# Value and forget-gate projections as one seven-product Strassen step, spatial mixing in plain fp32, and queries kept unnormalised, in a one-core decoder block

## The chip, the core and the metric

The kernel runs on one core of a Trainium2 chip. The metric is the device time of one execution in microseconds (us). Besides the timed runs there is one execution that was recorded by the hardware profiler; all rows of the profile and the trace come from that one. Its line numbers (L265) are those of the kernel before. Engines are named as in the profile: PE is TensorE (matmul), PEld its weight loads, DVE VectorE, ACT ScalarE, POOL GpSimd, SP the engine whose queue issues nearly all DMAs.

## The reference, cut to what matters

One decoder block, 1024 tokens by 1024 features, all float32:

```python
xn = rmsnorm(h, norm_mix_g)                 # 1024 tokens x 1024
proj = xn @ w_in                            # 1024 x 2568
q, k, v = proj[:, :512], proj[:, 512:1024], proj[:, 1024:1536]
log_f = log_sigmoid(proj[:, 2560:2568] + b_forget)     # 8 forget gates
att = forgetting_attention(q, k, v, log_f)  # softmax(q k^T / 8 + c_q - c_k, causal) v, 8 heads of 64
uv = gelu(proj[:, 1536:2560])               # u and gate, 512 columns each
sg = u * (w_spatial @ rmsnorm(gate) + b)    # per chunk of 128 tokens and group of 64 columns
h = h + concat(att, sg) @ w_out
h = h + conv_ffn(rmsnorm(h))                # up projection, causal convolution, silu gate, down
out = rmsnorm(h)
```

c is the running sum of log_f over the tokens. The change touches the projections of v and of the forget gates, the mixing `w_spatial @ ...`, and where q gets its per-token factor.

## The kernel before

**Products.** A float32 product is made of three fast matmuls (type fp32r): each operand is split into a high part (an ACT copy that rounds to fp32r) and a low part (a DVE subtraction, source minus high), and high x high, high x low and low x high are summed in PSUM. `tsplit` (L251) makes the two parts of a weight tile in a ring of six buffers (`ring`, L199: two tagged wy, four whl); `tmul` (L259) issues 4 x 3 matmuls for one of four 128-row blocks of the contraction, so that a product over 512 rows of contraction, for 512 tokens, is 48 matmuls. Their width is that of the weight tile: 512, 264 or 256 columns.

**Strassen steps.** With the two halves of the tokens and the two halves of the features, the input x is a 2 x 2 block matrix. The kernel keeps split blocks B11, B21 and B22 of it and the combinations T1 to T4, in the dictionary `XS`; tile tags H, V, x1, x2, t2, t3 hold them in turn. u and gate together (L284 to L419), queries and keys (`qk_step`, L594, four steps of 7 products of 12 matmuls 512 wide), the up projection and the down projection are each done with seven block products in place of eight.

**Values and forget gates before.** The 520 columns (512 values, 8 gates) are not done by a Strassen step, but as 8 products of 48 matmuls. Columns 0 to 255 of the values and the 8 gates (264 wide): `values_low` (L300) for the first half of the tokens, B11 and B21, interleaved block by block between the second and the third product of u and gate; `values_high` (L485) for the second half of the tokens, T3 and B22, behind u and gate; its weight sums are made on POOL (L487). Columns 256 to 511 (256 wide): T3, B11, B21, B22 (L810 to L850) behind the queries and keys, with weights `w0` split at L661 and the sums of L815 split at L845. `keep` (L304) copies the first results out of PSUM and writes them to DRAM (`vd`), `kept` (L696) loads them back; `evac_v` (L684) scales a result by the token's factor `rstd1` and splits it into the tile V (one ACT activation, one DVE operation for 256 columns of 128 tokens); all 16 are done ahead of the attention.

**Gate and mixing before.** `gate_part` and `gate_norm` (L465, L472) make the group norms of the gate and scale it, in the neighbourhood of `values_high`. `gate_gain` (L640) multiplies by the gain. `gate_split` (L667) splits the gate into high and low parts in four tiles of tag H; `spatial_weights` (L735) masks the mixing weights on POOL (L738) and splits them. `spatial` (L744) then issues for each of the 8 groups three fp32r matmuls 512 wide (L754 to L756), a DVE operation that adds the bias and multiplies with u (L759), and an ACT activation and a POOL product for the other half of the tokens. `turn_sg` (L775) transposes the result on PE (L780).

**Queries before.** In `emit` (L570) DVE multiplies queries and keys by the factor of the token (`rb`, a broadcast of rstd1 through DRAM, `rbd`, L403 to L405; queries also by -1/8), ACT makes the high part, DVE the low part, SP writes both to DRAM (`qd`, `kd`). `head_loads` (L823) brings them back per head. `logits_mm` (L914) makes the logits with a second matmul of 66 rows, of which rows 64 and 65 carry the running sums of the gates (`oned`, `ncd`); `logits_min` (L924) adds the causal mask and takes the row minimum in one DVE operation.

**What sets the order.** The framework orders each engine's instructions by a list schedule: by place in the program among those that it takes to be ready, and each queue then runs in that fixed order. `Line` (L30) overrides it: while `act.on` or `dve.on` is set, ACT or DVE runs its instructions in the order of the program, and `after` and `behind` put one instruction behind another without a wait between engines. Before the change this is on up to L402 and from L746 to L1060. `gates["keys"]` and `gates["queries"]` (L616, L633) are the last DVE operations on PSUM of the last query and key step; the splits of `w0` and `gate_gain` are put behind them. Buffers of one tag are reused in turn, and the DMA or instruction that writes a new tile waits for the last reader of the old one.

## Time and profile before

| | us |
|---|---|
| median of 3 runs (lowest, highest) | 1054.91 (1054.14, 1054.94) |
| profiled execution, its own time | 1053.8 |
| its span, first to last instruction | 1052.1 |
| PE busy | 1041.9 |
| DVE busy | 884.1 |
| ACT busy | 569.7 |
| POOL busy | 233.8 |
| u and gate, last two products (71.53 to 93.29) | 21.76 |
| `values_high` (93.29 to 104.92) | 11.63 |
| queries and keys (104.92 to 181.71) | 76.79 |
| columns 256 to 511 of the values (181.71 to 205.11) | 23.40 |
| mixing and first transposes (205.11 to 214.08) | 8.97 |

Times in the trace count from the start of the span. A row of the timeline gives start, duration, engine, line, operation, output and input tiles, and the number of instructions merged; the bracket at its end is the engine's idle time before it and what ended that. A row of the windows gives, for a stretch, its length, the busy time (and number of instructions) of each engine, the granted clock, the DMA share and GB/s. A row of the groups gives count, busy time and mean ns. A matmul's duration in a row is longer than its distance from the next one, because matmuls are pipelined; costs are therefore taken from the distance.

### The profile page before, as it was taken

Reading aid. Unit: us, or ns where it says so; the run is one execution under the profiler, and the core shown is the slowest. Engines: PE = TensorE matmul, PEld = TensorE weight load, DVE = VectorE, ACT = ScalarE, POOL = GpSimd, SP = SyncE. Lnnn points to the kernel's source line nnn. Section 1 sums busy time; section 2 is a strip of 40 time slices with the busy share of each in tenths; the row PEclk is TensorE's granted clock in tenths of the full one; section 3 lists DMA queues with packets and bytes.
Section 4 is the critical chain, followed back from the end, with each engine's and each line's share of the span. In section 5 each row is a group of like instructions: output and inputs, shape, how many; then the busy total and the mean of one; then the engine's idle time right before and its main releaser. Section 6 shows DMA issues by size and latency. Waiting matters only on the chain.

```text
span 1052.1 us, 14351 instructions
## 1 busy us (share of the span) xinstructions
PE 1041.9 (99%) x5037; PEld 873.8 (83%) x5037; DVE 884.1 (84%) x1293; ACT 569.7 (54%) x1008; POOL 233.8 (22%) x177
## 2 busy tenths in 40 slices
PE   9999999999999999999999999999999999999997
PEld 6989888988888888888888888888888888888886
DVE  6998797777787779998999989899897866997774
ACT  6777544456766746654344344444444554454654
POOL 0003231520421640253333423323331000000000
PEclk9999999999999999999999999999999999999999
DMA  9623456855755444222255332332322999333432
GB/s 332 214 8 134 139 154 172 230 145 181 191 159 163 152 163 157 80 90 90 80 180 170 120 113 78 131 120 69 131 82 80 316 329 303 103 100 100 144 119 98
DMA packets 67471, 155.77 MB, mean 148 GB/s; under 512 B 9060, under 2 KB 10036, under 8 KB 67400
## 3 DMA queue, kind: packets, MB, share of 16 engines
q1 hardware_dynamic: 66088, 154.82, 46.5%
q8 instruction: 39, 0.64, 0.3%
q14 instruction: 32, 0.26, 0.1%
q10 hardware_dynamic: 1312, 0.04, 0.1%
HBM read 111.96 MB, written 42.87 MB: 147 GB/s over the span
## 4 chain that ended last, share of the span: by engine, by line
PE 95%; DVE 2%; ACT 1%; issue 1%; DMA 0%; SPq 0%; ACTq 0%
PE k L1548 20%; PE qc L1288 11%; PE qa L1288 11%; PE qd L1288 11%; PE ps L265 6%; PE pb L265 5%; PE qb L1288 5%; PE pb L984 3%; PE pb L968 2%; PE qa L430 2%; PE qc L430 2%; PE qd L430 2%; PE pl L920 1%; PE pl L921 1%; PE pf L1008 1%; PE pf L1009 1%
## 5 line engine op out<-in xcount | busy, mean ns | idle before, releaser
L1548 PE MATMUL k<-whb,wha 128*128 128x512 f32 (+1 forms) x936 | 209.9, 386 | 0.0
L1548 PEld LDWEIGHTS k<-whb,wha 128*128 128x128 f32 x936 | 174.1, 188 | 35.8 <-DVE wha L161 0.2
L1288 PE MATMUL qc<-xT,whb 128*128 128x512 f32 x540 | 129.9, 389 | 0.2 <-ACT whb L155 0.2
L1288 PE MATMUL qa<-xB,wha 128*128 128x512 f32 x528 | 127.4, 390 | 0.0
L1288 PEld LDWEIGHTS qc<-xT,whb 128*128 128x128 f32 x540 | 101.3, 188 | 21.6 <-ACT whb L155 0.6
L1288 PEld LDWEIGHTS qa<-xB,wha 128*128 128x128 f32 x528 | 98.8, 188 | 20.8 <-DVE wha L161 0.4
L155 ACT CAST wha<-sg 128x512 fp32r<-128x512 f32 x77 | 47.7, 622 | 97.0 <-PE k L1548 86.5
L155 ACT CAST whb<-sg 128x512 fp32r<-128x512 f32 x82 | 50.6, 618 | 86.1 <-PE qc L1288 65.9
L161 DVE TENSOR_TENSOR wha<-sg,wha 128x512 fp32r<-128x512 f32 x77 | 52.7, 687 | 38.4 <-ACT wha L155 38.3
L1288 PE MATMUL qd<-xB,whb 128*128 128x512 f32 x264 | 63.7, 389 | 0.0
L1288 PE MATMUL qd<-xT,whb 128*128 128x512 f32 x264 | 63.7, 389 | 0.0
L969 ACT CAST pt<-pb 128x512 fp32r<-128x512 f32 x72 | 40.5, 585 | 41.5 <-PE pb L968 36.0
L1172 POOL TENSOR_TENSOR sg<-raw 128x512 f32<-128x512 f32 x20 | 30.8, 1539 | 139.9 <-DVE whb L161 79.9
L1288 PE MATMUL qb<-xT,whb 128*128 128x512 f32 x252 | 61.0, 389 | 0.0
L161 DVE TENSOR_TENSOR whb<-sg,whb 128x512 fp32r<-128x512 f32 x82 | 57.0, 697 | 4.4 <-ACT whb L155 4.3
L970 DVE TENSOR_TENSOR pt<-pb,pt 128x512 fp32r<-128x512 f32 x72 | 47.9, 688 | 15.1 <-ACT pt L969 15.0
L1288 PEld LDWEIGHTS qd<-xT,whb 128*128 128x128 f32 x264 | 49.5, 188 | 10.5 <-DVE u L1395 0.3
L1288 PEld LDWEIGHTS qd<-xB,whb 128*128 128x128 f32 x264 | 49.5, 188 | 10.3
L1288 PEld LDWEIGHTS qb<-xT,whb 128*128 128x128 f32 x252 | 47.2, 188 | 10.1 <-DVE whb L161 0.3
L984 PE MATMUL pb<-pt,V 128*128 128x512 f32 (+3 forms) x192 | 49.6, 362 | 0.4 <-DVE pt L970 0.3
L1175 POOL TENSOR_TENSOR sg<-sg,raw 128x512 f32<-128x512 f32 x20 | 33.3, 1665 | 63.4 <-DVE whb L161 63.4
L1173 POOL TENSOR_TENSOR sg<-sg,raw 128x512 f32<-128x512 f32 x20 | 35.1, 1757 | 47.2 <-issue 44.6
(417 smaller groups left out, 2267.0 us busy)
## 6 DMA issues: line engine op xcount, KB each, us to landing
raw<-wup SPq DMA_DIRECT2D x44, 512.0 KB
sg<-hx SPq DMA_DIRECT2D x77, 256.0 KB
hx<-hs SPq DMA_DIRECT2D x44, 256.0 KB
hx<-ca SPq DMA_DIRECT2D x35, 256.0 KB
xT<-wdn SPq DMA_DIRECT2D x28, 256.0 KB
x<-kd SPq DMA_DIRECT2D x24, 256.0 KB
A<-xtok SPq DMA_DIRECT2D x8, 512.0 KB
raw<-wqk SPq DMA_DIRECT2D x8, 512.0 KB
```

The costliest lines, as they stand in the source:

```text
L155: act.copy(h, src)
L161: return eng.tensor_tensor(out=l, in0=src, in1=f32(h), op=ALU.subtract)
L265: pe.matmul(banks[m], xs(n, xi, k)[:, ms], w[:, wi, :], start=(first and k == 0 and c == 0 and (own or m % 2 == 0)), stop=(k == 3 and c == ...
L430: pe.matmul(ps, w[:, wi, ks], xs(n, xi, k), start=(first and c == 0), stop=(c == 11), skip_group_check=True)
L969: casts.append(act.copy(pt[:, 0, :], ptr))
L970: los.append(dve.tensor_tensor(out=pt[:, 1, :], in0=ptr, in1=f32(pt[:, 0, :]), op=ALU.subtract))
L984: seq(pe.matmul(po[half][:, o:o + w], lhs, pt[:, s, c:c + w], start=(new and s == 0), stop=(s == 1 and (half, k) in ((1, 6), (0, 3))), ski ...
L1172: pool.tensor_tensor(out=s[0], in0=a21, in1=a22, op=ALU.add)
L1173: pool.tensor_tensor(out=s[1], in0=s[0], in1=a11, op=ALU.add)
L1175: pool.tensor_tensor(out=s[3], in0=s[1], in1=a12, op=ALU.add)
L1288: pe.matmul(ps, w[:, wi, ks], xb[:, xi, k, :], start=(first and n == 0), stop=(n == 11), skip_group_check=True)
L1548: pe.matmul((banks[bk + m] if ps is None else ps)[:, o], xh[:, xi, ms], wh[:, wi, o], start=((first and p_ == 0 or new) and n == 0), stop= ...
```

## The change: what it does

- **Values and forget gates become one Strassen step** of seven products. The two first, B11 and B21 (264 wide), stand where `values_low` stood, one after the other: the four blocks of B11, a copy of its result to DRAM (`vx[0]`), then the four of B21 into the same banks. Two, T3 and B22 (264 wide), stand where `values_high` stood; their weight sums are made by DVE (`vsum`) from tiles `va` and `v3rd` that hold both column halves of the weights (two loads of 128 x 1824 and one of 128 x 512 floats, in place of 1.1 MB), and their results go to DRAM (`vx[1]`, `vx[2]`). Three, T2, T4 and T1 (256 wide, `vmul`), stand behind queries and keys; their sums with the stored results (`xy`, `xl`, loaded back) give three blocks of values, two of which go through DRAM (`vu`).
- **Order.** DVE and ACT keep the program's order (`on`) also from L402 to the first query product; the gate norms, the splits and the subtractions are written out in one sequence there. The POOL sums for the first query weights are put behind the last low part of that sequence (`behind_`).
- **Mixing** takes the gate and the masked weights unsplit, as plain fp32: two matmuls 256 wide for each group in place of three fp32r ones 512 wide. `gate_split` and the split of the mixing weights go.
- **Queries** are no longer multiplied by the token's factor in `emit`; the factor (-rstd/8) is the scale of the DVE operation in `logits_min`, the mask changes sign, and the second logits matmul has 67 rows, with ncd rows prepared for both sides.
- **8 of the 16 `evac_v`** (heads 4 to 7) move into the attention, one in each of the steps 5 to 12.

```diff
-    values_low(0)
+    for k in range(2):
+        tmul(half(B), low_w(0, k), "B11", k, True)
     t2_of(0)
...
+    w12 = [low_w(1, k) for k in range(4)]
     for m in range(4):
         dve.tensor_tensor(out=ut[0][:, m, :], in0=S[m], in1=vgt[0][:, m, :], op=ALU.add)
-    values_low(3)
+    copies(B, vx[0])
+    for k in range(4):
+        tmul(half(B), w12[k], "B21", k, False)
...
-    act.on = dve.on = False
+    act.on = False
     rb = sb("t01", [P, 1024])
     act.dma_start(out=rbd.rearrange("a p -> p a"), in_=rstd1)
     sp.dma_start(out=rb, in_=rbd.rearrange("a b -> (a b)").unsqueeze(0).to_broadcast((P, 1024)))
+    act.on = True
+    gms = cst.tile([P, 64], F32, name="gms")
     XS["B22"] = xset(("t3", "t2"))
+    va = [sb("G", [P, 1824]) for _ in range(2)]
+    v3rd = sb("gg", [P, 512])
+    for i in range(2):
+        sp.dma_start(out=va[i], in_=wva[i])
+    sp.dma_start(out=v3rd, in_=wvk)
...
+    def vsum(i):
+        dve.tensor_tensor(out=own_[i][:, 0:3, 0:256], in0=oth[i], in1=own_[i][:, 0:3, 0:256], op=ALU.add)
+        dve.tensor_tensor(out=own_[i][:, 3, 0:256], in0=v3rd[:, 256 * i:256 * i + 256], in1=own_[i][:, 3, 0:256], op=ALU.add)
...
+    for k in range(4):
+        tmul(B, w4[k], "B22", k, False)
+    vsum(0)
+    sq = [square(1, 0), square(1, 2)]
+    w3 = [high(own_[0][:, k, :], 264) for k in range(2)]
+    reduce(sq[0], 1, 0)
     for m in range(4):
-        gelu(vgt[1][:, m, :], 4 + m)
         dve.tensor_tensor(out=vgt[0][:, m, :], in0=ut[1][:, m, :], in1=S[m], op=ALU.add)
         gelu(vgt[0][:, m, :], m)
+    for k in range(2):
+        low(w3[k], own_[0][:, k, :])
+    reduce(sq[1], 1, 2)
+    w3 += [high(own_[0][:, k, :], 264) for k in (2, 3)]
+    sq = [square(0, 0), square(0, 2)]
+    dve.tensor_tensor(out=va[1][:, 0:1056], in0=va[0][:, 0:1056], in1=va[1][:, 0:1056], op=ALU.add)
+    vsum(1)
+    for k in (2, 3):
+        low(w3[k], own_[0][:, k, :])
+    reduce(sq[0], 0, 0)
+    w4 = [high(own_[1][:, 0, :], 264)]
+    reduce(sq[1], 0, 2)
+    low(w4[0], own_[1][:, 0, :])
+    act.activation(gms, gms, AF.Sqrt, bias=eps[:, 0:1], scale=1.0 / 64)
+    dve.reciprocal(gms, gms)
+    S = [bank() for _ in range(4)]
+    for k in range(4):
+        tmul(half(S), w3[k], "T3", k, True)
+    w4.append(high(own_[1][:, 1, :], 264))
+    low(w4[1], own_[1][:, 1, :])
+    for m in range(4):
+        dve.tensor_tensor(out=ut[1][:, m, :], in0=B[m], in1=ut[1][:, m, :], op=ALU.subtract)
+    for k in (2, 3):
+        w4.append(high(own_[1][:, k, :], 264))
+        behind_ = low(w4[k], own_[1][:, k, :])
...
+    for hf in (1, 0):
+        for t in (0, 2):
+            norm(hf, t)
+    S2 = [sbank() for _ in range(4)]
+    for k in range(4):
+        tmul(half(S2), w4[k], "B22", k, True)
+    copies(S, vx[1], 1)
...
     W = [Weights(0)]
+    W[0].split("A11", "A12")
+    W[0].sums(behind_)
...
+    copies(S2, vx[2])
...
+    act.on = dve.on = False
...
-    def emit(t, dst, i, scale, parts):
+    def emit(t, dst, i, parts, src=None):
         for o in parts:
-            dve.scalar_tensor_tensor(out=t[:, 1, o], in0=t[:, 1, o], scalar=scale, in1=rb[:, o],
-                                     op0=ALU.mult, op1=ALU.mult)
-            act.copy(t[:, 0, o].bitcast(F32R), t[:, 1, o])
-            dve.tensor_tensor(out=t[:, 1, o], in0=t[:, 1, o], in1=t[:, 0, o], op=ALU.subtract)
+            if dst is kd:
+                dve.tensor_tensor(out=t[:, 1, o], in0=t[:, 1, o], in1=rb[:, o], op=ALU.mult)
+            x = t[:, 1, o] if src is None else src
+            act.copy(t[:, 0, o].bitcast(F32R), x)
+            dve.tensor_tensor(out=t[:, 1, o], in0=x, in1=t[:, 0, o], op=ALU.subtract)
...
+    l21, l22, l11 = (sb("raw", [P, 1024]) for _ in range(3))
+    for i, t in enumerate((l21, l22, l11)):
+        sp.dma_start(out=t, in_=wvl[i])
+    behind(dve.tensor_tensor(out=l21, in0=l21, in1=l22, op=ALU.add), "keys")
+    behind(dve.tensor_tensor(out=l11, in0=l11, in1=l21, op=ALU.add), "keys")
...
+    vw = {"S2": pairs(l11, "keys"), "A22": pairs(l22, "queries")}
     gate_gain(0)
+    xy = sb("x1", [P, 2, 1024])
+    xl = sb("pt", [P, 1024])
+    sp.dma_start(out=xl, in_=vx[0])
+    for i in range(2):
+        sp.dma_start(out=xy[:, i], in_=vx[1 + i])
+    dve.tensor_tensor(out=xy[:, 0], in0=xy[:, 0], in1=xl, op=ALU.subtract)
+    dve.tensor_tensor(out=xy[:, 1], in0=xy[:, 1], in1=xl, op=ALU.add)
...
-            pe.matmul(ps, ws[0][:, g, :], vgs[c][:, 0, j], start=True, stop=False)
-            pe.matmul(ps, ws[0][:, g, :], vgs[c][:, 1, j], start=False, stop=False)
-            m = pe.matmul(ps, ws[1][:, g, :], vgs[c][:, 0, j], start=False, stop=True)
+            for hf in range(2):
+                m = pe.matmul(ps[:, hf * 256:hf * 256 + 256], ws[:, g, :], vgt[hf][:, :, g * 64:(g + 1) * 64],
+                              start=(hf == 0), stop=(hf == 1), skip_group_check=True)
...
+    Q = [sbank() for _ in range(2)]
+    vmul(Q, vw["S2"], "T2")
...
+    act.on = dve.on = True
+    hw = [slice(0, 512), slice(512, 1024)]
+    for j, o in enumerate(hw):
+        dve.tensor_tensor(out=va_[:, o], in0=Q[j], in1=va_[:, o], op=ALU.add)
+        dve.tensor_tensor(out=vb_[:, o], in0=Q[j], in1=vb_[:, o], op=ALU.subtract)
+    vw["S1"] = pairs(l21)
+    Q = [sbank() for _ in range(2)]
+    vmul(Q, vw["A22"], "T4")
+    R = [sbank() for _ in range(2)]
+    vmul(R, vw["S1"], "T1")
+    for j, o in enumerate(hw):
+        dve.tensor_tensor(out=vc_[:, o], in0=va_[:, o], in1=Q[j], op=ALU.add)
+    sp.dma_start(out=vu[0], in_=vc_.rearrange("p (m c) -> p m c", c=256))
+    V.extend(sb("V", [P, 2, 8, 2, 64], F32R) for _ in range(2))
+    for j, o in enumerate(hw):
+        dve.tensor_tensor(out=vb_[:, o], in0=R[j], in1=vb_[:, o], op=ALU.subtract)
+        for m in (2 * j, 2 * j + 1):
+            evac_v(4 + m, 0, vb_[:, m * 256:m * 256 + 256])()
+        dve.tensor_tensor(out=va_[:, o], in0=va_[:, o], in1=R[j], op=ALU.subtract)
+    sp.dma_start(out=vu[1], in_=va_.rearrange("p (m c) -> p m c", c=256))
...
-        m = dve.tensor_tensor_reduce(out=places[h, i][jj], in0=ps[:, 0:n], in1=msk[:, 1024 - n:1024], scale=1.0,
+        m = dve.tensor_tensor_reduce(out=places[h, i][jj], in0=ps[:, 0:n], in1=msk[:, 1024 - n:1024], scale=ss1[:, j:j + 1],
...
+        if n == 2:
+            vh = sb("A", [P, 2, 4, 256])
+            sp.dma_start(out=vh, in_=vu.rearrange("h p m c -> p h m c"))
+        if 5 <= n < 13:
+            low = evac_v(n - 5, 1, vh[:, (n - 5) // 4, (n - 5) % 4, :])
+            after(tc, low(), los[-1])
+            after(tc, vhigh[0], exs[-1])
```

More of the change, by code (lines that the diff above doesn't have):

```diff
@@ L17 @@
 BIG = 3.0e38
+MASK = -1.0e30
 NFF = 22
@@ L298, in half, with low_w, copies @@
         return [b[:, 0:264] for b in banks]
[L300 to L305 removed]
+    def low_w(i, k):
+        return tsplit(wl[:, k, i, :] if k < 3 else wl3[i], n=264)
+    def copies(banks, dst, gate=None):
+        t = ring(F32).rearrange("p a c -> p (a c)")
         for m in range(4):
[L307 to L309 removed]
+            act.copy(t[:, m * 256:m * 256 + 256], banks[m][:, 0:256])
+            if gate is not None:
+                act.copy(zf[:, 4 * gate + m, 0:8], banks[m][:, 256:264])
+        sp.dma_start(out=dst, in_=t)
     def t2_of(j):
@@ L317, in t2_of @@
                                      op0=ALU.mult, op1=ALU.add)
-    values_low(0)
+    for k in range(2):
+        tmul(half(B), low_w(0, k), "B11", k, True)
     t2_of(0)
-    values_low(1)
+    for k in range(2, 4):
+        tmul(half(B), low_w(0, k), "B11", k, True)
     t2_of(1)
```

249 lines of the change are left out of this document (102 added, 147 removed).

## The prediction

> **What bounds the kernel now.** I read the page first, then the waits of PE, the busy time by windows between the seams of the stages, and the timeline at the two seams that the change touches.
>
> ```profile
> span 1052.1 us, 14351 instructions
> PE 1041.9 (99%) x5037; PEld 873.8 (83%) x5037; DVE 884.1 (84%) x1293; ACT 569.7 (54%) x1008; POOL 233.8 (22%) x177
> ...
> PE 95%; DVE 2%; ACT 1%; issue 1%; DMA 0%; SPq 0%; ACTq 0%
> ```
>
> The chain that ended last lies on PE for 95% of the span. So a matmul taken away is worth its distance to the next one, if nothing else becomes late; and the next in line is DVE at 84%.
>
> ```profile
> PE pb L968 <- DVE pt L970: 0.8, 2, 0.5
> ...
> 93.29:104.92 11.63, 11.63 (x97) 11.62 (x96) 10.09 (x13) 6.35 (x16) 4.24 (x4) 1.00 0.01 1
> 104.92:181.71 76.79, 76.79 (x344) 63.57 (x342) 62.13 (x99) 36.35 (x65) 22.30 (x15) 1.00 0.56 154
> 181.71:205.11 23.40, 23.29 (x193) 23.08 (x192) 18.76 (x32) 11.37 (x25) 8.16 (x8) 1.00 0.77 214
> ...
> 214.08:347.29 133.21, 132.39 (x768) 115.31 (x767) 104.98 (x215) 89.08 (x200) 28.42 (x27) 1.00 0.56 161
> ```
>
> The first row is a wait of PE on another engine, 0.8 us in two waits: nothing in the stages up to 214 us makes PE wait longer. In the windows the first column after the length is PE, the third DVE: PE is full throughout, and DVE has 1.5 us of 11.6 left behind u and gate, 4.6 of 23.4 in the last value products, 28 of 133 in the attention.
>
> **The change part by part.** *Value products.* Two rows of the timeline, 48 matmuls each, give the cost of one 256-wide product, and a third the wait ahead of them:
>
> ```profile
> 184.97 2.82 PEld L265 LDWEIGHTS ps<-whl,x 128*128 128x128 f32 x23 [0.32 <-DVE whl L44]
> 187.83 5.92 PE L265 MATMUL ps<-whl,V 128*128 128x256 f32 x48
> 193.59 5.92 PE L265 MATMUL ps<-whl,x 128*128 128x256 f32 x48
> 27.43 11.63 PE pb L265 x96
> ```
>
> From 187.83 to 193.59 are 5.76 us, 0.120 us for each matmul. Four products with that wait are the 23.40 us of the window; three are 17.3. Removed: **6.1 us**. The other four products stay 264 wide (last row: 96 in 11.63 us, 0.121 each, two products), in other places: nothing on PE.
>
> *Between B11 and B21* ACT now copies each bank before PE adds to it.
>
> ```profile
> 42.51 0.36 ACT L51 COPY whl<-pb 128x256 f32<-128x256 f32 x1
> ```
>
> One copy of that size took 0.36 us; PE is meanwhile in the three other banks, 9 matmuls or 1.09 us. Hidden; without that cover it would be four copies, 1.4 us.
>
> *Mixing.* Before, 24 matmuls stand between these two rows of the chain, 5.47 us:
>
> ```profile
> 205.28 0.23 PE pb L754
> ...
> 210.75 1.75 PE ps L780 x16
> ```
>
> After, 16 matmuls in plain fp32, 256 wide. No row shows one. The nearest is the fp32 transposition (second row): 16 of 128 columns in 1.75 us, 0.11 each, so 0.22 for 256 columns and 3.5 us in all. That is the lower end. But a transposition passes one operand through, while a product of two unsplit numbers needs at least the partial products for which this kernel now issues three fp32r matmuls, with low x low four. Four at half the distance of a 512-wide one (0.228 / 2) make 0.456 us, 7.3 us in all: the upper end. I take the upper one for that reason: **+1.8 us**; the lower one would be -2.0.
> The Trainium skill, FP8 and Floating Point Precision, TensorE Precision Notes, states for true fp32 four passes through the array; by the four passes the sum is the one taken, by the transposition's row 3.8 us less on PE, and no run yet shows which.
>
> *First seam, behind u and gate.* DVE now runs one fixed order whose first step needs `va[0]` and `v3rd`. How late do these land? SP's queue and the DMA rates before:
>
> ```profile
> 69.22 0.80 SPq L414 DMA_DIRECT2D G<-wv x2
> 76.87 0.33 SPq L405 DMA_DIRECT2D t<-rbd x1
> 77.25 1.53 SPq L414 DMA_DIRECT2D G<-wv x2
> 83.80 1.48 POOL L487 TENSOR_TENSOR G<-G 128x264 f32<-128x264 f32 x2 [1.22 <-DMA G<-wv]
> ...
> SPq L405 <- DMA rbd<-rstd: 6.8, 1, 6.8
> ...
> 78.00:79.00 1.00, 1.00 (x6) 0.82 (x5) 1.00 (x2) 1.00 (x2) 0.00 (x0) 1.00 0.36 27
> 79.00:80.00 1.00, 1.00 (x6) 0.83 (x5) 0.84 (x2) 1.00 (x3) 0.00 (x0) 1.00 0.89 276
> 82.00:83.00 1.00, 1.00 (x6) 0.84 (x5) 1.00 (x3) 0.00 (x0) 0.58 (x1) 1.00 1.06 404
> ```
>
> SP stands 6.8 us at L405, behind the scatter of rstd1 to DRAM; until 79 little moves (27 GB/s), then 276 to 404 GB/s, and the last old weights arrive at 83.80. I expect `va[0]` (0.93 MB) ahead of L405 and `va[1]` (0.93) and `v3rd` (0.26) behind the 0.52 MB of `rb`: 2.65 MB. Until 79 some 0.2 MB got through before; the packets of `va` are 3.5 times as long (7296 for 2112 bytes), so up to 0.7 MB now. The rest, 1.95 to 2.45 MB at 404 GB/s, lands at 83.8 to 85.1. I take 83.5, the early end, since long packets also spare the slow start at 276. From there DVE's order runs:
>
> ```profile
> 80.10 2.35 DVE L44 TENSOR_REDUCE gms<-pt 128x16 f32<-128x1024 f32 x2 [0.26 <-ACT pt L44]
> 89.83 0.35 ACT L44 ACTIVATE gms<-gms,eps 128x64 f32<-128x64 f32 x1
> 90.21 0.55 DVE L44 RECIPROCAL gms<-gms 128x64 f32<-128x64 f32 x1 [0.24 <-ACT gms L44]
> 92.04 2.48 DVE L44 TENSOR_TENSOR A<-ps,A 128x512 f32<-128x512 f32 x4
> 100.18 4.62 DVE L44 TENSOR_TENSOR G<-G,gms 128x1024 f32<-128x1024 f32 x4
> 29.31 0.77 DVE L51 TENSOR_TENSOR wy<-A,wy 128x264 fp32r<-128x264 f32 x2
> ```
>
> Sum of the last block 0.4, four reductions 4.7, eight PSUM additions and subtractions 2 x 2.48, eight low parts of 264 columns 3.1, weight sums of 1056, 768 and 256 columns 1.2 + 1.3 (in proportion to 512 and 1024), root and reciprocal 0.9, four norms 4.62, the low part of A11 0.7: 21.9 us, to 105.4. PE wants that low part with its second matmul behind 104.92, at 105.15. Wait: **+0.2 us**; 0 if the loads land by 83.2, 1.8 at 85.1, more if `va[0]` also falls behind L405 (0.93 MB, 2.3 us). Queued behind the waiting DVE instruction is everything named, and PE behind that.
>
> *Queries and keys.* Eight multiplications by the token's factor (DVE) and three copies (ACT) go:
>
> ```profile
> L44 DVE TENSOR_TENSOR G<-G 128x512 f32<-128x512 f32 x4 | 2.7, 680 | 0.7 <-ACT G L44 0.7
> L44 DVE SCALAR_TENSOR_TENSOR G<-G,t 128x512 f32<-128x512 f32 x3 | 2.0, 680 | 0.0
> ```
>
> That is 8 x 0.68 us of DVE, but PE never waits in this window (76.79 of 76.79): nothing. The two forms cost the same, so I price the per-token scale in `logits_min` at nothing too, and the 67th row of the second logits matmul likewise (columns set its length). If the scale did cost, it would lie on the DVE work of the attention.
>
> *Second seam, behind queries and keys.* PE wants the weights of T2 at 181.71, of T4 at 187.5 and of T1 at 193.2. DVE may start with them behind this row:
>
> ```profile
> 176.47 0.69 DVE L44 TENSOR_TENSOR G<-G,qd 128x512 f32<-128x512 f32 x1
> 198.83 0.47 ACT L44 ACTIVATE V<-ps,rstd 128x256 fp32r<-128x256 f32 x1 [0.26 <-PE ps L265]
> L51 DVE SCALAR_TENSOR_TENSOR V<-ps,rstd,V 128x256 fp32r<-128x256 f32 x4 | 1.9, 483 | 1.8 <-ACT V L51 1.8
> L51 DVE SCALAR_TENSOR_TENSOR A<-pb,cp,A 128x256 f32<-128x256 f32 x7 | 3.2, 479 | 0.6 <-PE pb L756 0.6
> ```
>
> From 177.2: sums of T2's weights 2.3 (1024 columns at 4.62 / 4), five key steps and two query steps of 0.62 (2.48 / 4), six low parts 3.7, the gain 2.3, the two differences `xy` 2.3, four operations on the first product's bank 2.5: 17.4 us, to 194.6, and T1's first low part 0.6 earlier, at 194.0. Wait ahead of T1: **+0.8 us**; 2.7 if the four low parts of `kept` (1.9) come first, 0 if PE takes the first mixing groups meanwhile. T2's own weights: sums and one low part are ready by 181.8 if they go first, 2.0 us later if the key steps do; I take 0.
> Behind T1 the fixed order has, on its first bank (done 1.4 us ahead of the end) and then the second: subtraction 0.62, two ACT activations (0.47) with two DVE low parts (0.48), subtraction 0.62. By these, DVE reaches the first mixing result 4.2 us behind the end of T1. PE meanwhile fills its four free banks (3.6 us), and the fifth group waits until 4.7: **+1.1 us**, 0 if groups run ahead of T1.
>
> *Attention.* Eight `evac_v` are added there, 0.48 us of DVE and 0.47 of ACT each. The 133.21 us of the window hold some 36 steps of 3.7 us, with 0.78 us of DVE and 1.2 of ACT idle in each: hidden, nothing.
>
> **Sum:** -6.1 + 1.8 + 0.2 + 0.8 + 1.1 = -2.2 us. The profiled execution took 1053.8 us by its own time (1.7 around its span); the median of the runs shown is 1.1 above that, 1054.91. So 1051.6 by the one, **1052.6 us** by the other, which is the forecast.
>
> **Rivals.** *DVE becomes the bound at both seams (slower).* For it: 84% busy, one fixed queue, each step waiting for the one ahead. Loads at 86.3 (no more let through than before, and 1.2 us behind other traffic) give 3.0, T2's weights 2.0, T1's 2.7, the tail 1.1: -4.3 + 8.8 = +4.5, 1059.4. It is slower by 0.2% from 6.4 us of waits in all. Against: DVE's work in the second stretch is about what it was. Going: eleven 512-column steps (6.8), the split of the mixing weights (1.2), four low parts of 256 columns (1.6), eight evacuations (3.8), 13.4 us; coming: the sums (2.3), six low parts (3.7), `xy` (2.3) and ten steps on the products' banks (6.2), 14.5. *The moved evacuations fall on the attention's chain (slower):* if each pair is in the way, 8 x 0.95 = 7.6, 1060.2; half of them, 1056.4. From 4.3 us on it is slower. Against it the idle time above. *All waits hidden:* -4.3, 1050.6; for it that PE now waits next to nowhere. *Mixing at the transposition's pace:* DVE's eight operations (0.48 each) behind 4.2 us set the end 8.0 us behind T1, for 8.4: 1052.2, and with no waits at all 1046.8. *The gain is given back to waits:* 4 us of them, 1054.6.
>
> **Chances.** Forecast 0.36 (between 1051.4 and 1053.8), all hidden 0.18, transposition's pace 0.08, given back 0.15, DVE bound 0.14, attention 0.09. What a measurement of this kernel can tell from no change is about 0.2%, 2.1 us, so faster is below 1052.8: 0.24 of the forecast, all hidden and the pace, 0.50; within it 0.12 + 0.15 = 0.27; slower 0.23. The range for 8 in 10 leaves out the far ends of the pace and of both slower cases: 1049.6 to 1058.8.
>
> **What would show it.** Right: 48 matmuls fewer in three products of 5.76 us from the end of queries and keys; 0.45 us between two mixing matmuls; T3's values right behind u and gate with the first query product within 0.5 us of its old start; eight evacuations in the attention with no PE wait on them. Wrong: PE waits on DVE low parts at A11 or S1 above 2 us (the late load or DVE's queue), waits on `evac_v` in the attention, mixing at 0.22 us, or stages beyond 365 us that change.

## The result, and the profile after

The changed kernel takes 1066.93 us (median of 4 runs, 1064.73 to 1069.66), the kernel before 1054.93 (4 runs, 1054.14 to 1055.67): ratio 1.0115, 95% interval 1.009 to 1.014. It is slower by 12 us, where I forecast 2 us faster, and outside the range that I gave. The profiled execution took 1066.44, its span is 12.6 us longer than that of before.

The head of the page and the start of its chain of waits, to be held against the first fence of the prediction:

```profile
span 1064.7 us, 14262 instructions
PE 1043.8 (98%) x4997; PEld 873.1 (82%) x4997; DVE 892.9 (84%) x1298; ACT 564.2 (53%) x1003; POOL 223.5 (21%) x169
...
PE 83%; DVE 8%; ACT 4%; DMA 2%; issue 2%; SPq 0%; POOL 0%; ACTq 0%; DVEq 0%
```

PE is busy for 1.9 us more although it has 40 matmul records fewer, and the chain leaves PE for 17% of the span in place of 5%. Two things happened: PE waits, and for a while it works slower. The waits of PE (us in total, times, longest):

```profile
PE pb L792 <- ACT pt L52: 3.3, 1, 3.3
PE pb L1015 <- DVE pt L1017: 1.8, 2, 0.9
PE ps L267 <- DVE A L52: 1.5, 1, 1.5
PE ps L845 <- DVE whl L52: 1.3, 1, 1.3
```

Before, no wait of PE behind the first 10 us was above 0.6 us. By stages (windows of the changed kernel, cut where the same products begin; first the length):

```profile
94.60:110.59 15.99, 14.33 (x98) 13.45 (x96) 15.88 (x25) 12.04 (x27) 0.51 (x1) 0.89 0.09 34
110.59:189.20 78.61, 77.15 (x344) 63.62 (x342) 60.18 (x95) 32.52 (x58) 23.30 (x16) 1.00 0.60 172
189.20:208.86 19.66, 17.81 (x146) 17.34 (x145) 16.27 (x25) 5.06 (x12) 3.44 (x5) 1.00 0.88 239
208.86:223.40 14.54, 10.83 (x67) 9.36 (x65) 11.41 (x19) 7.79 (x18) 9.81 (x13) 1.00 0.53 170
223.40:377.70 154.30, 150.49 (x872) 130.47 (x873) 127.28 (x251) 107.01 (x240) 40.71 (x40) 0.99 0.59 173
```

Against before: behind u and gate 15.99 for 11.63 (+4.4; DVE busy in 15.88 of it), queries and keys +1.8, the last value products 19.66 for 23.40 (-3.7 where -6.1 was removed), mixing and transposes 14.54 for 8.97 (+5.6), attention 154.30 for 150.94 (+3.4). The first 70 us add 1.3 by a late load at the start; with the same instructions there, e2_mix began T4 at 71.67 and before at 71.53, so I count that as chance. Behind the attention nothing changed.

The first window also shows a granted clock of 0.89. Cut finer:

```profile
105.00:106.00 1.00, 1.00 (x6) 1.00 (x6) 1.00 (x2) 1.00 (x5) 0.00 (x0) 0.50 0.00 0
...
107.00:108.00 1.00, 1.00 (x6) 1.00 (x6) 1.00 (x2) 1.00 (x3) 0.00 (x0) 0.51 0.20 78
```

For 3.4 us PE ran at half its clock, which costs 1.7 us of work, while its column of busy time shows nothing. A second such stretch lies at 285.5 to 288.9. Before had none until the last 3 us of its span (1049 to 1052).

### The profile page after: what moved, and what is told of

Same layout as the page of the kernel before. It is cut to its first block, busy times and chain, and to the rows that moved or that the text cites. A ratio compares the mean times of both kernels' runs of the same rounds, so it can differ in the third digit from the quotient of the medians.

```text
span 1064.7 us, 14262 instructions
## 1 busy us (share of the span) xinstructions
PE 1043.8 (98%) x4997; PEld 873.1 (82%) x4997; DVE 892.9 (84%) x1298; ACT 564.2 (53%) x1003; POOL 223.5 (21%) x169
## 4 chain that ended last, share of the span: by engine, by line
PE 83%; DVE 8%; ACT 4%; DMA 2%; issue 2%; SPq 0%; POOL 0%; ACTq 0%; DVEq 0%
PE k L1602 20%; PE qc L1342 11%; PE qa L1342 11%; PE qd L1342 11%; PE qb L1342 5%; PE pb L1031 2%; PE pb L1015 2%; PE ps L267 2%; PE pl L967 1%; PE pl L968 1%; PE pf L1055 1%; PE qc L515 1%; PE pf L1056 1%; PE pf L1057 1%; PE qd L515 1%
```

## The experiments

The theory after the result: DVE, now bound to one order, is late at each seam for a reason of that seam (a late load, an order with other work ahead, POOL beside it), and PE's waits there are partly paid twice, by the half clock. The rivals: DVE simply has too much to do, so that a wait taken away returns at the next place; the pointer scale lengthens the attention; the plain fp32 mixing brings the loss. Differences below are taken between ratios to the kernel before, at 1054.5 us; the changed kernel is 1.0115. Its own interval (1.009 to 1.014, four runs 5 us apart) is the widest part of these differences: against another kernel of four runs a difference below some 3 to 4 us is not clear of the noise, and there the traces carry the argument.

### e1_loads: va and v3rd land early

```diff
+    w3 = [high(own_[0][:, k, :], 264) for k in range(2)]
     rb = sb("t01", [P, 1024])
     act.dma_start(out=rbd.rearrange("a p -> p a"), in_=rstd1)
...
     W = [Weights(0)]
+    sp.dma_start(out=rb, in_=rbd.rearrange("a b -> (a b)").unsqueeze(0).to_broadcast((P, 1024)))
```

> The changed kernel with one thing altered: the scatter of rstd1 to DRAM and its broadcast (needed only for the keys) are issued behind the loads of va, v3rd and the first query weights, in place of ahead of va[1] and v3rd. Theory A (the late load sets the first seam, and the half clock follows from PE's wait): va and v3rd land before 81.4, where DVE begins to wait in the changed kernel, its waits of 1.6 and 5.4 us go, PE's waits of 0.2 and 1.5 us in the two value products go, the granted clock stays at 1.00 from 104 to 108, and the first query product begins 4.4 us earlier; some of the 1.8 us of the first query step goes with it. Together 4.4 to 6.2 us less than the changed kernel's 1066.9: about 1061. Rival B (DVE's own 21.9 us of work in its fixed order are too much whenever the loads come): PE still waits on DVE for more than 1 us there, and at most 1.5 us are won: 1065.4 or more.

Measured: 1061.37, ratio 1.0067 (1.0052 to 1.0082), 5.1 us less, which is clear of the noise: theory A. First the changed kernel, SP's queue and DVE there, then the same of e1_loads:

```profile
70.75 0.33 SPq L418 DMA_DIRECT2D G<-wva  x1
80.10 0.33 SPq L411 DMA_DIRECT2D t<-rbd  x1
80.52 0.38 SPq L418 DMA_DIRECT2D G<-wva  x1
80.99 0.38 SPq L419 DMA_DIRECT2D gg<-wvk  x1
81.47 0.38 SPq L524 DMA_DIRECT2D raw<-wqk  x1
...
82.93 0.96 DVE L52 TENSOR_TENSOR G<-G 128x768 f32<-128x768 f32 x1 [1.57 <-DMA G<-wva]
89.32 0.43 DVE L52 TENSOR_TENSOR G<-gg,G 128x256 f32<-128x256 f32 x1 [5.43 <-DMA gg<-wvk]
```

```profile
70.09 2.67 SPq L413 DMA_DIRECT2D G<-wva  x2
74.16 0.33 SPq L414 DMA_DIRECT2D gg<-wvk  x1
...
80.63 0.95 DVE L52 TENSOR_TENSOR G<-G 128x768 f32<-128x768 f32 x1
81.50 0.42 DVE L52 TENSOR_TENSOR G<-gg,G 128x256 f32<-128x256 f32 x1
...
99.82 3.07 PE L267 MATMUL ps<-wy,t 128*128 128x264 f32 x24
102.73 3.07 PE L267 MATMUL ps<-whl,t 128*128 128x264 f32 x24
105.64 2.88 PE L512 MATMUL qc<-V,whl 128*128 128x512 f32 x12
```

The bracket of 5.43 us is gone, DVE goes on 7.8 us earlier, and the two halves of the second value product take 2.91 us each with no bracket: the seam is back at 11.63 us (94.01 to 105.64), queries and keys at 77.5.

### e12_order: only the broadcast moved

```diff
     act.dma_start(out=rbd.rearrange("a p -> p a"), in_=rstd1)
-    sp.dma_start(out=rb, ...)                       # ahead of va[1]
...
     W = [Weights(0)]
+    sp.dma_start(out=rb, ...)
```

> The changed kernel with only the broadcast of rb moved behind the weights of the first queries in SP's queue; the scatter of rstd1 (1024 pieces of 4 bytes) stays where it was, from 67.7 on. It takes e1_loads apart: there both were moved. Theory A (the scatter itself starves the other transfers: 26 GB/s from 70 to 80 in the changed kernel, 434 from 72 to 74 in e1_loads): the loads of va[1] and v3rd are issued at 73 to 75 but move at some 26 GB/s until 78 to 80; then 2.1 MB, and the query weights beside them, need until 84 to 86, so DVE still waits 2 to 4 us, PE waits 0.5 us or more in the second value product, and half of the gain of e1_loads comes: 1063.5 to 1065. Rival B (the wait of SP's queue at the broadcast was the whole harm): the loads land by 81.5 as in e1_loads, DVE doesn't wait, and the time is that of e1_loads, 1061.4.

Measured: 1065.26, ratio 1.0093 (1.0067 to 1.0119), 2.3 us less by the middles (the four runs spread from 1063.17 to 1068.41, so the time alone proves little). In the loads it is theory A. Windows (last column: GB/s) and queues of the changed kernel, then a window and DVE in e12_order, then a window in e1_loads. The second fence is the transfer page of the changed kernel from 67 to 80 us; its row is ACT's queue with the scatter: packets, MB and share:

```profile
70.00:80.00 10.00, 10.00 (x46) 8.28 (x45) 10.00 (x16) 5.16 (x8) 0.00 (x0) 1.00 0.69 26
80.00:84.00 4.00, 4.00 (x20) 3.30 (x19) 2.31 (x3) 2.58 (x5) 0.00 (x0) 1.00 0.83 285
84.00:89.30 5.30, 5.30 (x25) 4.40 (x24) 0.00 (x0) 0.69 (x2) 0.00 (x0) 1.00 1.00 400
```

```profile
q10 hardware_dynamic: 1040, 0.00, 3.6%
```

```profile
76.00:78.00 2.00, 2.00 (x10) 1.69 (x9) 2.00 (x5) 0.03 (x1) 0.00 (x0) 1.00 0.94 40
...
87.04 0.43 DVE L52 TENSOR_TENSOR G<-gg,G 128x256 f32<-128x256 f32 x1 [1.99 <-DMA gg<-wvk]
```

```profile
72.00:74.00 2.00, 2.00 (x10) 1.66 (x9) 2.00 (x3) 0.62 (x1) 0.00 (x0) 1.00 1.09 434
```

From 70 to 80 us the core's DMA moves 26 GB/s in the changed kernel and 22 in e12_order, where the loads are issued within 2.6 us of their time in e1_loads (72.63 to 70.09), but behind the scatter (40 in its best two microseconds). In e1_loads, with the scatter behind the loads, it is 240 over the same 10 us and 434 in the best two. As only the scatter's place differs between e1_loads and e12_order here, the scatter is the cause. How it holds the others back stays open: its 1040 packets are recorded from 68 to 70, and the slow stretch lasts until SP's queue, which waits for the scatter, goes on at 80.10; in e1_loads loads still moved at 266 GB/s from 84 to 86, beside 810 of those packets. The PE wait that I expected in the second value product was not there, since in this execution PE came to the seam 1.3 us later by two other waits (0.84 at 51 us, 0.50 at 63); instead PE waited 0.74 and 0.97 us in the first query step, and a stretch of half clock followed (124 to 128).

### e4_fill and e9_fill3: work in the waits

```diff
+    for i in range(12):
+        pe.matmul(S[i % 4][:, 264:512], xs("T3", 0, 0)[:, 0:P], w3[3][:, 0, 0:248], ...)
     S2 = [sbank() for _ in range(4)]
...
+    idle(bank(), 14, xs("T1", 0, 0)[:, 0:P], ...)          # e9_fill3 only
     vmul(R, vw["S1"], "T1")
...
+            if g == 4:
+                idle(sbank(), 27, xs("T1", 0, 0)[:, 0:P], ...)   # e9_fill3 only
```

> The changed kernel with twelve more matmuls (248 wide, into the unused half of banks, their results used by nobody) between the two value products behind u and gate, where PE stands idle for 1.5 us. Theory A (the fall of the granted clock to half from 104.5 to 108 us is the answer to that idle time, and it is a cost of its own): the filler lies in the wait and costs next to nothing, the clock stays at 1.00, the second value product takes 3 us in place of 5, and the first query product begins 1.5 to 1.9 us earlier, 1065.2. Rival B (the clock falls for another reason, or the idle time wasn't idle): the clock still reads about 0.5 and the time is the same or up to 1.5 us longer.

Measured: 1065.16, ratio 1.0103 (1.0088 to 1.0118), 1.3 us less by the middles. The intervals overlap, so by itself this is weak. The trace has no stretch of half clock, and the first query product begins 2.0 us earlier (108.57), as in theory A. But e2_mix and e3_evac, which leave this seam as it is in the changed kernel, show no stretch there either; e3_evac:

```profile
100.73 3.79 PE L267 MATMUL ps<-wy,t 128*128 128x264 f32 x24 [0.53 <-DVE A L52]
107.26 0.62 PE L515 MATMUL qc<-V,whl 128*128 128x512 f32 x2
```

So a trace without a stretch doesn't show that the filler prevented it. What these traces do give is the price of a stretch: from the first T3 product to the first T2 product of the values, e2_mix takes 93.2 us, e3_evac 93.1 and e4_fill 93.2 without one, the changed kernel 94.6 and e10_seam2 95.4 with one. So a stretch goes with 1.4 to 2.3 us more there, near the 1.7 of its halved rate. The profiled execution of the changed kernel also shows the first seam at its dearest: 15.99 us, against 13.11 in e2_mix and 13.03 in e3_evac, which pay a part of the difference in the first query step.

> The changed kernel with filler matmuls, whose results nobody uses, in its three largest waits outside the attention: 12 (248 wide) between the two value products behind u and gate, 14 (256 wide) ahead of the product T1, 27 (256 wide) between the fourth and the fifth mixing group. No wait is shortened; PE only works through 1.3 + 1.5 + 2.9 us of them. Theory A (the half clock is a second cost of those waits): the mean granted clock of the runs rises from 0.996 to 0.998, as only the attention's two waits are left, the runs lie closer together, and the time is 1.7 to 3.4 us less: 1064. Rival B (the clock falls whatever PE does there, or the spread of the runs has another cause): the clock stays at 0.996 and the time is the same or up to 1 us longer.

Measured: 1064.25, ratio 1.0092 (1.0079 to 1.0106), 2.4 us less with 53 matmuls more; the mean granted clock of its runs is 0.997 to 0.999 (changed kernel 0.996 to 0.997), their spread 2 us in place of 5. That is what theory A forecast, but the two intervals still overlap. One stretch of half clock is left in its profile, at 125 to 128, behind a wait of 1.85 us in the first query step that no filler covers; in e4_fill the same wait of 1.84 us drew none.

The plainest evidence lies between runs of one kernel. Those of e3_evac took 1060.94, 1061.05, 1062.63 and 1066.80 us at mean granted clocks of 0.999, 0.998, 0.997 and 0.993: from first to last 0.006 of the clock, some 6 us of full speed, for 5.9 us of time.

### e3_evac: the moved splits elsewhere in the attention

```diff
-        if 5 <= n < 13:
-            low = evac_v(n - 5, 1, vh[:, (n - 5) // 4, (n - 5) % 4, :])
+        if 12 <= n < 20:
+            low = evac_v(n - 12, 1, vh[:, (n - 12) // 4, (n - 12) % 4, :])
```

> The changed kernel with the eight splits of the values of heads 4 to 7 moved from the steps 5 to 12 of the attention to the steps 12 to 19, away from the stretch from 274 to 287 us in which POOL splits weights. Theory A (DVE and ACT meet POOL's splits there, PE waits 0.95 and 0.73 us, and the clock falls to half behind it): both waits and the half clock go, 3.5 us of the attention come back but for what the moved splits cost in their new place: about 1063.5. Rival B (the scale by a pointer in logits_min, 64 times some 60 ns, sets it, or the wait was POOL's alone): PE waits and a low clock stay near 284 and the time stays within 1 us of 1066.9.

Measured: 1061.84, ratio 1.0085 (1.0059 to 1.0111), 3.2 us less by the middles; the intervals overlap. The evidence is the trace: the attention is 151.48 us (changed kernel 154.30, before 150.94). Of the eight moved splits of the changed kernel three ran between 275 and 287 us, beside POOL's work, in 0.62, 1.56 and 0.96 us in place of 0.48. POOL and DVE there:

```profile
279.44 2.54 POOL L163 TENSOR_TENSOR whl<-raw,whl 128x512 fp32r<-128x512 f32 x2
280.70 1.56 DVE L737 SCALAR_TENSOR_TENSOR V<-A,rstd,V 128x256 fp32r<-128x256 f32 x1 [1.69 <-ACT V L733]
282.92 0.66 PE L1015 MATMUL pb<-ident,t 128*128 128x128 f32 x4 [0.95 <-DVE pt L1017]
284.78 0.50 PE L967 MATMUL pl<-x 128*128 128x512 f32 x1 [0.73 <-DVE mn L980]
```

ACT is late with the high part (it makes four others for the same weights first), DVE waits 1.69 us, its low part takes 1.56 us beside POOL's split (0.48 elsewhere), the next transposed low parts are behind it in DVE's queue, and PE waits. In e3_evac PE's only wait from 275 to 292 is 0.23 us, and there is no stretch of half clock: theory A in the attention. Its slowest run (1066.80 at a clock of 0.993) points to such stretches in other executions.

### e6_ptr and e7_mixonly: two parts alone, on the kernel before

```diff
-        m = dve.tensor_tensor_reduce(..., scale=1.0,
+        m = dve.tensor_tensor_reduce(..., scale=one[:, 0:1],
```

> The kernel before with one thing altered: the scale of the operation in logits_min comes from a column of ones in place of the constant 1.0. It computes the same. Theory A (some 60 ns more for each of 64, 3.9 us of DVE in the attention, most of it beside PE's work): the attention is 0 to 0.6 us longer, 1054.9 to 1055.2. Rival B (the pointer is what lengthens the attention by 2.7 us, and e3_evac won by keeping other work out of its way): 1.5 us or more longer, 1056 or more, with PE waits on the minima.

Measured: 1054.79, ratio 1.0001 (0.9992 to 1.0010): theory A. The same operation, first before, then e6_ptr:

```profile
L933 DVE CUSTOM_DVE_ANT_0 wy<-pl,t,lim 128x512 f32<-128x512 f32 x8 | 5.9, 742 | 0.0
```

```profile
L933 DVE CUSTOM_DVE_ANT_0 wy<-pl,t,lim 128x512 f32<-128x512 f32 x8 | 6.4, 801 | 0.0
```

It does cost 59 ns each, and the attention hides them.

```diff
-            pe.matmul(ps, ws[0][:, g, :], vgs[c][:, 0, j], start=True, stop=False)
-            pe.matmul(ps, ws[0][:, g, :], vgs[c][:, 1, j], start=False, stop=False)
-            m = pe.matmul(ps, ws[1][:, g, :], vgs[c][:, 0, j], start=False, stop=True)
+            for hf in range(2):
+                m = pe.matmul(ps[:, hf * 256:hf * 256 + 256], ws[:, g, :], vgt[hf][:, :, g * 64:(g + 1) * 64], ...)
```

> The kernel before with only the mixing altered: gate and masked weights unsplit, two plain fp32 matmuls 256 wide for each group in place of three fp32r ones 512 wide, and the splits of the gate and of the weights gone. Theory A (the mixing by itself costs its 16 matmuls at 0.43 to 0.45 us, 6.9 us in place of 5.47, and no wait, and the stall in the changed kernel is that of the values' subtractions and splits ahead of it): 1.4 us longer, 1056.0. Rival B (the plain fp32 mixing brings the stall with it, since its results come in another rhythm): 3 us or more longer, with PE waits in the mixing above 1 us. Rival C (the eight splits of the gate and those of the weights that go were in the way of the values' splits): no longer than before.

Measured: 1055.80, ratio 1.0010 (1.0001 to 1.0019): 1.1 us more, the mixing's 16 matmuls in 6.90 us, no PE wait there. Theory A.

### e2_mix and e10_seam2: the order behind the last value product

e2_mix: each group's operation, then one of the eight others. e10_seam2 has a second order, and the kept values behind T1's weights:

```diff
-    kept()                                          # splits of the kept values
+    vkept = kept()                                  # only the load
...
     vw["S1"] = pairs(l21)
+    for m in range(4):
+        evac_v(m, 0, vkept[:, m, :])()
...
             if g < 7:
                 second()
+            rest(g)    # g 0-3: one subtraction; g 2-5: a high part; g 4-7: the low part of two groups ago
```

> The changed kernel with another order of DVE and ACT in the mixing: each group's bias-and-product operation comes as soon as its two matmuls are done, and one of the four subtractions or one of the four value splits stands behind each of the eight, in place of all eight ahead of the first group. Theory A (the 3.3 us stall before the fifth mixing group is the fixed order's): the stall goes, mixing takes 7.3 us in place of 10.4, and 3.3 us less in all: 1063.6. Rival B (the work is only moved: the transposes then wait for the two banks of T1, or the first logits for DVE): the logits begin less than 1 us earlier and the time stays within 1 us of 1066.9.

Measured: 1067.33, ratio 1.0116 (1.0101 to 1.0131), no gain: rival B. The stall in the mixing went, and another came:

```profile
206.34 7.07 PE L792 MATMUL pb<-G,pt 128*128 128x256 f32 x32
213.25 1.65 PE L816 MATMUL ps<-ident,A 128*128 128x128 f32 x12
218.47 1.11 PE L816 MATMUL ps<-ident,A 128*128 128x128 f32 x4 [3.56 <-DVE A L52]
...
215.13 0.90 DVE L52 SCALAR_TENSOR_TENSOR V<-x,rstd,V 128x256 fp32r<-128x256 f32 x1 [0.94 <-ACT V L52]
```

The 16 plain fp32 matmuls (two records each) run through in 6.91 us; but I had put each low part right behind its high part, so that DVE waited 0.94 us for ACT three times, each time behind an operation of ACT that waits for DVE.

> The changed kernel with only the second seam altered, as in e5_all: the low parts of the kept values behind those of T1's weights, and the second order of the mixing. Theory A (the seam's waits of 1.3 and 3.3 us and a part of the half clock are its own): 4.6 us less by the waits and about 0.8 by the clock, 1061.5. With e1_loads (5.4 less) and e3_evac (3.4 less by the interval's middle) that makes up the 11.6 us between the changed kernel and e5_all. Rival B (the seam's waits only pass on what the first seam delayed): less than 2 us won, 1065 or more.

Measured: 1063.60, ratio 1.0085 (1.0071 to 1.0098), 3.2 us less, between the two theories and just clear of the noise. T1's wait and the mixing's stall are gone, but a wait of 1.5 us for the masked mixing weights (POOL) and 1.0 us for POOL's products in the transposes stand in their place.

### e5_all, e8_best and e11_best: together

e5_all is e1_loads, e3_evac and e10_seam2 in one.

> The changed kernel with four things altered together: the loads of va and v3rd ahead of the scatter of rstd1 (as in e1_loads), the splits of heads 4 to 7 in the steps 12 to 19 (as in e3_evac), the low parts of the kept values behind those of T1's weights on DVE, and a second order in the mixing: each group's operation first, behind it one subtraction (groups 0 to 3) or one low part (groups 4 to 7) whose high part ACT made two groups earlier, since in e2_mix DVE waited 0.94 us three times for a high part made just ahead of it. Theory A (the change's gain on PE is real, and what ate it are these waits with the half clock behind them): no PE wait above 0.8 us from 80 to 350, no stretch of half clock in most executions, first query product at about 105.6, first logits at about 214.5 (changed kernel 223.4), attention 151.5 long: 1053.5, within 0.3% of the kernel before. Rival B (DVE has become the bound of these stages, so that a wait taken away at one place comes back at the next, as in e2_mix): the first logits stay behind 218 and the time above 1057.

Measured: 1055.30 (11 runs), ratio 1.0006 (0.9997 to 1.0015), 11.5 us less than the changed kernel; the three alone gave 5.1, 3.2 and 3.2, the same sum, each of them uncertain by 3 to 4 us. The time lies between the two theories, nearer to A (1053.5); the attention takes 151.5 us and the first logits begin at 216.57. No stretch of half clock in its profile, clocks of 0.998 to 1.000 in its runs. What PE still waited for:

```profile
PE pb L813 <- POOL A L799: 1.4, 2, 0.7
...
PE pb L267 <- DVE whl L52: 0.8, 1, 0.8
...
PE qc L512 <- DVE G L45: 0.6, 1, 0.6
PE ps L843 <- DVE whl L45: 0.5, 1, 0.5
```

The second row is the wait at 51 us; e8_best and e12_order have it too.

e8_best loads the mixing weights and the output weights earlier and makes T2's sums earlier:

```diff
+    ws = spatial_weights()
     head_loads(0)
-    ws = spatial_weights()
...
-    behind(dve.tensor_tensor(out=l21, in0=l21, in1=l22, op=ALU.add), "keys")
+    behind(dve.tensor_tensor(out=l21, in0=l21, in1=l22, op=ALU.add), "early")   # behind the last step's T3 product
```

> e5_all with three things more: the mixing weights are loaded ahead of the first head's queries and keys (PE waited 0.33 us for their mask), the weights for the gated half's output are loaded ahead of the store of the first value block (POOL's splits of them, and behind these its products, were late: two PE waits of 0.72 us in the transposes), and DVE makes the weight sums of T2 behind the last T3 product of queries and keys, where it stood idle (PE waited 0.50 us for the second low part). Theory A (what is left of the change's loss is such waits): those 2.3 us of waits go and the time is 1053.0, 2.3 less than e5_all and 1.5 less than before, since three value products fewer by one (5.8) less the dearer mixing (1.4) are worth 4.4 and some 3 us of waits stay. Rival B (each wait removed uncovers the next, as DVE and POOL are full there): less than 1 us won, 1054.3 or more.

Measured: 1055.02, ratio 1.0006 (0.9997 to 1.0015): rival B. The 0.33 and 0.50 us went, POOL's two waits stayed. One of its 11 runs took 1059.12 us at a mean clock of 0.994.

e11_best takes POOL's splits behind its products, and one squaring of ACT in u and gate behind the weights:

```diff
-                after(tc, x, splits[0])             # product behind the first split
...
-        squares(*((3,) if k == 2 else ()))
+    squares(3)
     copies(B, vd, 0)
```

> e8_best with two orders altered. POOL multiplies the second half of the mixing results ahead of its splits of the output weights, in place of behind the first of them (PE waited 0.70 and 0.72 us for these products in e8_best). And ACT squares the fourth block of tokens behind the high part of T2's last weights in u and gate, in place of ahead of it: in e5_all and e8_best that squaring waited 2.4 to 2.8 us for its load, which now shares the DMA queues with the store of B11's result, and PE waited 0.8 and 0.5 us behind it. Theory A (the loss that is left lies in such waits, each on its own): the two POOL waits and the two waits near 51 and 63 us go, 2.0 to 2.7 us, and the time is 1052.6, faster than before by 0.2%. Rival B (the next in line is as late: DVE's low parts of the turned half, the splits that fill the first steps of the attention): less than 1 us, 1054 or more, with new waits of the same sum.

Measured: 1053.89 (11 runs), ratio 0.9996 (0.9987 to 1.0005): 0.4 us below before and 1.1 below e8_best, by the middles, between the two theories; a gain over before is not shown. POOL's two waits and those at 51 and 63 us are gone from its trace. Its stages:

```profile
93.88:105.50 11.62, 11.62 (x97) 11.62 (x96) 9.77 (x16) 8.31 (x21) 1.55 (x1) 1.00 0.30 92
105.50:183.05 77.55, 76.96 (x343) 63.65 (x342) 62.63 (x96) 32.63 (x58) 22.25 (x16) 1.00 0.62 179
183.05:200.32 17.27, 17.27 (x145) 17.27 (x144) 14.33 (x21) 4.52 (x9) 3.95 (x5) 1.00 0.87 215
200.32:212.19 11.87, 10.79 (x67) 9.43 (x65) 10.74 (x20) 8.34 (x19) 7.81 (x11) 1.00 0.54 195
212.19:364.62 152.43, 149.59 (x873) 128.95 (x873) 125.85 (x251) 106.80 (x239) 42.40 (x42) 1.00 0.61 181
```

The three value products take 17.27 us with PE busy throughout, 6.1 less than before. What eats it: mixing and transposes +2.9 (1.4 of it the mixing's own), attention +1.5, queries and keys +0.8. So even with the large waits mended the gain on PE is nearly used up. The attention, for one, has 125.9 us of DVE work where before had 119.7:

```profile
214.08:365.02 150.94, 149.00 (x875) 129.32 (x874) 119.68 (x244) 104.18 (x233) 40.76 (x40) 1.00 0.56 163
```

## Why the prediction was wrong, point by point

**The step that failed first** is the one on the loads behind u and gate: "lands at 83.8 to 85.1. I take 83.5 ... Wait: +0.2 us". `v3rd` was used at 89.32. Up to 80 only 0.26 MB moved (26 GB/s for 10 us), not 0.7; from there the 2.4 MB left ahead of and including `v3rd` would need until 87.1 (285, then 400 GB/s). The sum also left out the 2.1 MB of the first query weights, issued 0.5 us behind it: by 89.3 some 3.5 MB had moved, 0.9 of them these, so they shared the engines instead of standing behind. The row I read (27 GB/s until 79) was in the prediction with its cause, the scatter; I let "long packets" outweigh it, and they moved less: 26 GB/s from 70 to 80, before 49. The 83.5 that I took lies below both of my own bounds, which the working doesn't support. The rival's bound, 86.3, was too early as well (86.87 in e2_mix, the earliest use with these loads). PE's wait also came one product earlier than the term had it: not at A11's low part, but at the second value product, behind DVE's four subtractions. e1_loads shows the price: 5.1 us, with the half clock and 1.1 us of the first query step, for 0.2 forecast.

The rival "DVE becomes the bound at both seams" (chance 0.14) named this wait, the one ahead of T1 and the tail; its 1059.4 lacks the half clock and the attention, and its loads and tail are too small.

**The attention** ("hidden, nothing") cost 3.4 us, for which I had a rival with a chance of 0.09. The mean idle time of a step (0.78 us of DVE) was no argument: three of the eight splits fell on the steps in which POOL and ACT prepare weights. e3_evac's trace shows it: elsewhere they leave 0.5 us of the 3.4. The pointer scale was not free per operation (59 ns), but cost no time (e6_ptr).

**The second seam.** PE waited 1.3 us ahead of T1 (0.8 forecast) and 0.5 at T2 (0 taken, 2.0 the other end). That 1.3 is near 0.8 is partly luck: the term took T1's low part to come ahead of those of the kept values, and the order was the other one, for which the prediction had 2.7:

```profile
198.18 1.90 DVE L45 SCALAR_TENSOR_TENSOR V<-wy,rstd,V 128x256 fp32r<-128x256 f32 x4
```

T1's low part follows at 202.40. In the mixing PE waited 3.3 us for 1.1. The place (fifth group) was right; two things were undersized. DVE reached the first mixing result 5.85 us behind the end of T1 (208.86) in place of 4.2, since two low parts beside POOL's split took 2.65 us in place of 0.96 (the terms that the prediction names there add up to 3.9, not 4.2; the waits of 0.58 us for ACT's high parts were in them as 0.47). And the bank came free only behind ACT's activation on it, some 0.5 us later, which the term left out:

```profile
211.54 2.65 DVE L52 SCALAR_TENSOR_TENSOR V<-x,rstd,V 128x256 fp32r<-128x256 f32 x2 [0.58 <-ACT V L52]
...
214.71 1.65 DVE L52 SCALAR_TENSOR_TENSOR A<-pb,cp,A 128x256 f32<-128x256 f32 x4
```

**The half clock** is in no part of the forecast. By the halved rate its two stretches are 3.4 us of the profiled 12.6.

**Right:** three products at 17.3 us (e11_best 17.27); mixing at 0.43 us a matmul (6.91 / 16; 0.456 taken, 0.22 the other end); no wait of PE for the copies between B11 and B21; queries and keys not shortened by the eight multiplications that went. The 0.43 us are 3.6 times the 0.12 of an fp32r matmul of the same width, near the four passes that the Trainium skill (FP8 and Floating Point Precision, TensorE Precision Notes) gives for true fp32.

**Right only in part.** Queries and keys, forecast to stay the same, keep 0.8 us more in e11_best. PE waits 0.6 us in the first query step on DVE, whose operations on the forget gates come later than before (at 115.96 in e1_loads, 110.12 before). And the result of B11, once copied, is stored to DRAM: in e5_all, e8_best and e12_order PE waits some 0.8 and 0.5 us at 51 and 63 us, behind a squaring of ACT whose load lands late. That this store delays the load was argued and not tested alone.

## What to carry to other kernels

Where PE is full and the next engine at 84%, a saving on PE is worth what the next engine's order lets through in that very stage; sum that engine's queue from the arrival of its last input, and count everything that shares the DMA engines, small-piece scatters first. Work "hidden" in mean idle time must be placed in named steps, away from those in which another engine prepares weights. And look at the granted clock around each new wait, since a wait of 1.5 us with a stretch of half clock behind it costs 3.

## What the runs showed of the hardware

- **Half clock after waits.** In the profiled executions, their last 3 us set aside, each stretch lasted 3.4 us at 0.50: two in the changed kernel, one each in e1_loads (behind the 3.3 us stall in the mixing), e2_mix (behind the 3.6 us), e9_fill3 and e10_seam2 (near 125), two in e12_order; none in before, e3_evac, e4_fill, e5_all, e6_ptr, e7_mixonly, e8_best and e11_best. It followed a wait of 1.5 us in the changed kernel, and waits of 0.74 and 0.97 us in e10_seam2 and e12_order, but not the changed kernel's stall of 3.3 us in the mixing. Which wait draws one stays open. The Trainium skill (TensorE: Matmul & The Clock Gate, Part 1 and Why this matters for your kernels) says that an idle window of about 3.4 us returns the clock to half and a busy one of that length to full, and asks for no PE-idle gaps above some 3 us. The length of the stretches agrees; that gaps of 1.5 us and less were followed by one does not, and the measurement decides.
- **A scatter of 4 KB in 4-byte pieces** held the loads behind it to 22 to 26 GB/s from 70 to 80 us (240 with the scatter issued behind them, 434 at best). The Trainium skill (DMA: Bandwidth & Descriptors, Rules for kernel authors) says that such a pattern becomes one descriptor for each element, which agrees with the 1040 packets under 512 bytes from 67 to 80 us for 1024 elements. That other queues starve beside it only these runs show.
- **DVE beside POOL:** the 256-column split took 0.48 us alone, 1.56 us beside a POOL split in the attention, and 2.65 us for two of them in the mixing.
